# First weights, early splits of the output rows, one column group of the softmax scaling on ScalarE, and gate's half folded into the values

## The chip, the core and the metric

The kernel runs on one core of a Trainium2 chip. Its time is the device time of one execution in microseconds (us). The engines that matter here are TensorE (PE, with its weight loads shown as PEld), VectorE (DVE), ScalarE (ACT), GpSimd (POOL) and SyncE (SP), which issues nearly all DMAs.

## What is computed

One layer of a hybrid encoder on 2048 tokens, a grid of 32 rows by 64 columns, of width 1024, in float32:

```python
h = rmsnorm(x, g)                              # 2048 x 1024
q, k, v, gate = split(h @ w_in, 4, axis=-1)    # w_in: 1024 x 4096
# 16 heads of 64: each token attends to 8 rows x 16 columns of the grid
# around it, with a learned bias per head and offset
s = einsum(q, k_window) * scale + bias         # NEG_INF outside the window
p = softmax(s)
o = einsum(p, v_window)
x = x + (o * silu(gate)) @ w_out               # w_out: 1024 x 1024
return rmsnorm(x, norm_f)
```

silu(gate) is gate/2 times (1 + tanh(gate/2)). The kernel keeps gate times (1 + tanh(gate/2)); the factor one half is applied elsewhere, and the change moves that place.

## The kernel before

**Arithmetic.** Every large product is made of three matmuls: each operand is rounded into a high part and a low part (high minus the rest), and high by high, high by low and low by high are added up in PSUM. So every operand is "split" first: usually ScalarE rounds (`wh`, `h`, `qh`, `gh`, `woh` by a Copy) and VectorE subtracts (`wl`, `l`, `ql`, `gl`, `wol`).

**Stages.** *Stage one* projects the first 1024 tokens. It starts with the values: `load_v0` (L529) and `load_x` bring in blocks of weights (two of 256 columns, a=0 and a=1; a block b holds two rows of blocks k) and of x; `split_v` (L537 the high part, L538 the low part) and `split_to` (L519) split them, and `values_of` (L555) multiplies, block k after block k, into four banks `pv`. The first block k=0 is done in two halves of 256 tokens. The rest of stage one and *stage two* (the other half of the tokens) use a scheme with seven products (L434); parts of stage two's projections are kept back.

*The attention loop* has 32 steps m and a last one. A step handles one pair of heads p and one band of rows T, in the order (p, 0) for eight p, (p, 1) and (p, 2) for eight p each, (p, 3) for eight p. Its instructions are written out in a fixed order, which is the order in each engine's queue. In step m:

1. `begin` sets up loads for later, `feed` emits a first stretch of filling matmuls;
2. `normalise(2m-1)` takes the reciprocal of the row sums (VectorE, L1040) and scales the second pair of column groups of the step before (GpSimd, L1044: two column groups j by two heads s);
3. `split_q` splits the next q (L519, L520), and three "turns" follow: `consume` splits the next item of weights, w_out's pieces in the later half (L194 high, L195 low), and `feed` emits filling matmuls;
4. `tables` adds bias and mask for a new type of row (GpSimd, L987), then one more turn and a last stretch of filling;
5. `turns(m-1)` transposes the probabilities (TensorE, L1101) and copies them out of PSUM (L1077, half on ScalarE, half on VectorE), then come the scores of step m (TensorE L1021, VectorE L1029, ScalarE's exponential with its sum L1035, GpSimd's L1044 for the first pair) and the products with the values (L1123).

**Filling.** `feed(n)` takes n matmuls from `projections()` (the projections kept back, L378 to L382) and, when those are used up, from `outputs()`, which multiplies the gated attention by w_out: per output tile n of 128 rows and half j of the columns 24 matmuls into a bank `po` (L1322 high by high, L1324 low rows by high weights, L1326 high rows by low weights), then `add_rows` adds x (L1220) and squares, and after the second half `finish` brings the root (L1237 on) and the scaling of the final norm (L1252). `amount[m]` is the filling of a step: 28 matmuls, later 53, in the last step 24; the stretches of a step get shares of it. `outputs()` calls `ahead` after each group of three matmuls: it loads rows of gated attention for coming tiles (`load_og`), and splits tile n (`split_og`, ScalarE's `gh` L1187, VectorE's `gl` L1188, two operations of 512 columns each) when its place is near. `clock` counts filling matmuls; a piece that has been loaded is only used when the clock has moved on by a threshold (32 for weights, 28 for rows).

Of the kernel before, what the change touches and what calls it, by code (L numbers as in the profile page):

```python
# [70 lines left out]
def build(ctx, tc, x, xr, xt, wg, rpb, last, w_out, n0, nf, masks, out):  # L71
# [58 lines left out]
    onesr = one.tile([128, 128], F32R, name="onesr")  # L130
    rt = one.tile([128, 16], F32, name="rt")
    g0 = one.tile([128, NK], F32, name="g0")
    accs = [one.tile([128, 512], F32, name=f"acc{i}") for i in range(2)]
# [24 lines left out]
    def load_item(it):  # L158
        kind, a, b = it
        t = raws[it] = raw([128, 512], F32, "raw")  # L160
        asked_at[it] = clock[0]
        if kind == "x":
            nc.sync.dma_start(t, xt[a * 128:(a + 1) * 128, b * 512:(b + 1) * 512])
        elif kind == "w":
            nc.sync.dma_start(t, wg[a[0], :, 512 * b:512 * b + 512])
        else:
            nc.sync.dma_start(t, w_out[a * 128:(a + 1) * 128, b * 512:(b + 1) * 512])
# [38 lines left out]
    def stats(c):  # L206
        ss = rows.pop(c)
        m = tiny.tile([128, 8], F32, name="m")[:, :4]
        nc.vector.tensor_tensor(m, ss[:, 0:8:2], ss[:, 1:8:2], OP.add)
        nc.vector.tensor_scalar(m, m, 1.0 / D, EPS, op0=OP.mult, op1=OP.add)  # L210
        rsqrt(rt[:, 4 * c:4 * c + 4], m, 4)

    dgs = {}
# [48 lines left out]
    AHEAD = 5  # L262
    clock = [0.0]
    freed = set()
    state = dict(used=0, loaded=0, half=-1, done_halves=0, event=0.0)
# [22 lines left out]
    def consume(n, asked=False, turn=False):  # L288
        for _ in range(n):
            load_ahead()  # L290
            if attending[0] and not asked and not turn:
                return
            if state["used"] == len(items) or not may_use(items[state["used"]]):
                return
            if attending[0] and clock[0] - asked_at[items[state["used"]]] < 32 and not asked:
                return
            it = items[state["used"]]
            state["used"] += 1
            use_item(it)
# [88 lines left out]
    def evac_v(u, t, p):  # L388
        v = ev([128, 512], F32, "v")
        nc.scalar.activation(v, p, AF.Copy, scale=rt[:, t:t + 1] if t < 8 else 1.0)  # L390
        dst = vd[u].rearrange("h n d -> n h d")[t * 128:t * 128 + 128]
        written.add(("v", u, t))
        store(("v", u, t), 8, lambda: nc.sync.dma_start(dst, v.rearrange("p (h d) -> p h d", h=4)))
# [136 lines left out]

    def split_v(u, a, b, ks=(0, 1)):
        t = VR[u, a, b].rearrange("p (k c) -> p k c", c=256)
        if a == 0 and ks[0] == 0:
            W[u, b] = wp([128, 2, 512], F32R, "wh"), wp([128, 2, 512], F32R, "wl")
        s, k = slice(a * 256, a * 256 + 256), slice(ks[0], ks[-1] + 1)
        h, l = W[u, b][0][:, k, s], W[u, b][1][:, k, s]
        nc.scalar.activation(h, t[:, k], AF.Copy)  # L537
        nc.vector.tensor_tensor(l, t[:, k], h.bitcast(F32), OP.subtract)  # L538
        if (a, ks[-1]) == (1, 1):
            for a in range(2):  # L540
                del VR[u, a, b]
# [24 lines left out]
    def stage_one():  # L566
# [108 lines left out]
        for b in (1, 2, 3):  # L675
            for a in range(2):
                load_v0(0, a, b, ev([128, 512], F32, "raw") if b == 3 else None)
            for k in (2 * b, 2 * b + 1):
                load("x%d1" % (k // 4 + 1), k % 4)
        for k in range(4):  # L680
# [5 lines left out]
        for k in range(NK):  # L686
            if k == 0:
                for h in range(2):
                    split_to(*(t[:, parts_[h]] for t in X1["B11"][0]), land["x11"][0][:, parts_[h]], gain("x11", 0))
                    if h == 0:  # L690
                        split_v(0, 0, 0, (0,))
                        split_v(0, 1, 0, (0,))
                    values_of(X1, 0, (2 * h, 2 * h + 1), (0,))
                continue
            elif k == 1:
                split_v(0, 0, 0, (1,))
                split_v(0, 1, 0, (1,))
            elif k % 2 == 0:
                split_v(0, 0, k // 2)
                split_v(0, 1, k // 2)  # L700
            f = "x%d1" % (k // 4 + 1)
            split("B" + f[1:], land[f][k % 4], k % 4, f)
            values_of(X1, 0, (0, 1, 2, 3), (k,))
# [82 lines left out]
    def stage_two():  # L786
# [9 lines left out]
        def also(n, i):  # L796
            if n == 0:
                if i == 0:
                    load_ahead()
                    load_e(0, xp)[0]()  # L800
                elif i == 1:
                    load_e(0, xp)[1]()
                    load_masks()
# [166 lines left out]

    def load_e(p, pool_=None):
        def rows(s):
            t = (pool_ or ep)([128, 512], F32, "e")[:, :480]
            E[p, s] = t.rearrange("p (u v) -> p u v", v=32)
            nc.sync.dma_start(t, rpb[2 * p + s])

        return [lambda: rows(0), lambda: rows(1)]
# [59 lines left out]

    def normalise(i):
        st = ST.pop(i)
        nc.vector.reciprocal(st[:, 8:12], st[:, 4:8])  # L1040
        for j, C in enumerate(pairs[i][2]):
            for s in range(2):
                o = 8 + 2 * j + s
                nc.gpsimd.tensor_scalar(X[i, C][s], X[i, C][s], st[:, o:o + 1], 0.5, op0=OP.mult, op1=OP.mult)  # L1044

# [234 lines left out]
    ready = dict(loaded=2, split=1, res=RES_EARLY)  # L1280

    def outputs():
        loaded_at = {1: -1e9}

# [4 lines left out]
        def ahead(k, i=0):  # L1289
            n = ready["loaded"]  # L1290
            if n < tiles and place[n] <= k + 4 and og_ready(n):
                load_og(n)
                loaded_at[n] = clock[0]
                ready["loaded"] += 1
            if ready["res"] < min(squared[0] + RES_BUFS, k + 3, len(turns_)):
                more_rows()
            n = ready["split"]
            near = 2 if quiet[0] else -1
            if n < ready["loaded"] and place[n] <= k + near and clock[0] - loaded_at[n] >= 28 and whole(n):
                split_og(n)  # L1300
# [77 lines left out]
    def begin(m):  # L1378
# [11 lines left out]
        if m == 0:  # L1390
            bias(0, 0, 2)
            later_loads(load_e(order[1][0]), 5, 3)

# [17 lines left out]
    for m in range(cycles + 1):  # L1411
        a = amount[m]
        begin(m)
        feed(a * 0.35)
        if m:
            normalise(2 * m - 1)
        middle(m)
        if m:
            quiet[0] = True
            for k in range(3):  # L1420
                consume(1 + (m == 1), turn=True)
                feed(a * 0.11)
                if k == 1:
# [3 lines left out]
            if quiet[0]:  # L1427
                consume(1, turn=True)
                feed(a * 0.12)
                quiet[0] = False  # L1430
            else:
                feed(a * 0.12)
        else:
            feed(a * 0.45)
        feed(a * 0.2, 8)
        if m:
# [11 lines left out]
        if m:  # L1448
            values(2 * m - 2)
            values(2 * m - 1)  # L1450
        n = next_sums(m)
        if 0 < m and n and order[m][1] < 2:
            for f in load_e(order[n][0]):
                f()
# [52 lines left out]
```

## Time and profile before

| | |
|---|---|
| median of 3 runs | 1062.33 us (1062.28 to 1062.53) |
| profiled execution | 1062.42 us, of which the span of the profile is 1060.6 |
| TensorE busy | 1048.6 us (99%), granted clock 0.9 or more in each slice |
| VectorE / ScalarE / GpSimd busy | 725.7 (68%) / 518.5 (49%) / 312.9 (30%) us |
| normalising on GpSimd, L1044 | 256 instructions, 176.1 us |
| DMA | 207.58 MB, mean 196 GB/s |

"Busy" is the time in which an engine works on an instruction; issuing a DMA or waiting is not counted. In a list of waits a row reads: engine, the waiting group, what released it, the total wait, how often, the longest. In a timeline a row reads: time from the span's start, duration, engine, line of the kernel, operation, output<-inputs, their shapes and types, xN for N instructions of one kind in a row, and in brackets the idle time ahead of it with what released it. A row of a window reads: the window, its length, then the busy time (and number of instructions) of PE, PEld, DVE, ACT and POOL in it, the granted TensorE clock, the busy share of the DMA engines and GB/s. A row of the groups reads: line, engine, operation, shapes, number | busy time, mean ns of one | idle time ahead and its releaser.

### The profile page before, as it was taken

To read this page: it belongs to the slowest core of one execution; us is meant where nothing else is said; L and a number is where in the kernel's file an instruction comes from. 1 tells how busy PE (TensorE), PEld (TensorE's weight loads), DVE (VectorE), ACT (ScalarE), POOL (GpSimd) and SP (SyncE) were. 2 spreads that over 40 slices of the span, in tenths; PEclk is the share of its full clock that TensorE was granted. 3 is DMA by queue.
4 is the path that set the end of the run, shared out by engine and by line. 5 is a ranking of instruction groups with operands and counts; after the bars stand their busy time and mean duration, and the time that the engine had idled before them with its cause. 6 is when DMAs were issued, how large, how long until landed. Compare 5 with 4: busy or idle time off the path is not lost.

```text
span 1060.6 us, 20997 instructions
## 1 busy us (share of the span) xinstructions
PE 1048.6 (99%) x7608; PEld 877.1 (83%) x7608; DVE 725.7 (68%) x1593; ACT 518.5 (49%) x1218; POOL 312.9 (30%) x392
## 2 busy tenths in 40 slices
PE   8999999999999999999999999999999999999997
PEld 6888888887888888888888888888887888888886
DVE  5476888768897625666576667766778777686654
ACT  7645344333343334333265656666767656445422
POOL 0000221322311000000157775665756642213200
PEclk9999999999999999999999999999999999999999
DMA  8733655353635433533798778886987788777352
GB/s 309 227 100 108 190 202 179 126 149 119 184 120 154 120 100 89 170 99 129 234 300 262 239 238 246 269 268 207 297 280 251 222 282 273 255 243 247 105 155 80
DMA packets 129184, 207.58 MB, mean 196 GB/s; under 512 B 11768, under 2 KB 55544, under 8 KB 129080
## 3 DMA queue, kind: packets, MB, share of 16 engines
q1 hardware_dynamic: 128648, 205.84, 62.5%
q8 instruction: 60, 0.98, 0.4%
q10 hardware_dynamic: 432, 0.40, 0.1%
q14 instruction: 44, 0.36, 0.1%
HBM read 147.47 MB, written 58.72 MB: 194 GB/s over the span
## 4 chain that ended last, share of the span: by engine, by line
PE 91%; DVE 4%; issue 1%; POOL 1%; DMA 1%; ACT 0%; SPq 0%; POOLq 0%; DVEq 0%
PE pp L434 30%; PE pv L555 16%; PE s L1021 7%; PE o L1123 7%; PE po L1324 5%; PE po L1326 5%; PE po L1322 5%; PE pp L382 4%; PE pp L378 4%; PE pp L380 4%; PE ph L1101 4%; DVE f L417 1%; POOL x L1044 1%; DMA land<-in_xt_dram 1%; POOL em L987 1%
## 5 line engine op out<-in xcount | busy, mean ns | idle before, releaser
L1044 POOL TENSOR_SCALAR x<-x,st 128x360 f32<-128x360 f32 (+5 forms) x256 | 176.1, 706 | 222.9 <-DVE st L1040 205.0
L434 PE MATMUL pp<-h,f 128*128 128x512 f32 x576 | 186.6, 390 | 0.0
L1035 ACT ACTIVATE x<-x,st 128x360 f32<-128x360 f32 (+5 forms) x256 | 151.3, 593 | 23.7 <-DVE st L1029 23.7
L454 POOL TENSOR_TENSOR tmp<-tmp,rb 128x512 f32<-128x512 f32 x36 | 58.6, 1628 | 270.1 <-DVE tmp L452 209.4
L987 POOL TENSOR_TENSOR em<-e,mk 128x264 f32<-128x264 f32 (+3 forms) x94 | 78.0, 864 | 192.1 <-DMA mk<-in_masks_dram 189.4
L434 PEld LDWEIGHTS pp<-h,f 128*128 128x128 f32 x576 | 108.2, 188 | 22.2
L1029 DVE CUSTOM_DVE_ANT_0 x<-s,em 128x360 f32<-128x360 f32 (+5 forms) x256 | 123.8, 538 | 0.6 <-POOL em L987 0.6
L434 PE MATMUL pp<-t,f 128*128 128x512 f32 x480 | 121.7, 390 | 0.3
L434 PE MATMUL pp<-l,f 128*128 128x512 f32 x288 | 112.2, 389 | 0.0
L434 PEld LDWEIGHTS pp<-t,f 128*128 128x128 f32 x480 | 90.0, 188 | 19.6 <-DVE u L447 1.1
L1324 PE MATMUL po<-woh,gl 128*128 128x512 f32 x252 | 99.2, 394 | 1.5 <-DVE gl L1188 1.5
L1326 PE MATMUL po<-wol,gh 128*128 128x512 f32 x252 | 98.9, 393 | 0.0
L1322 PE MATMUL po<-woh,gh 128*128 128x512 f32 x252 | 98.9, 393 | 0.0
L1077 DVE COPY pta<-ph 120x512 f32<-120x512 f32 (+5 forms) x96 | 57.8, 641 | 55.4 <-PE ph L1101 55.4
L555 PE MATMUL pv<-wh,h 128*128 128x512 f32 x256 | 88.4, 391 | 1.9 <-ACT h L519 1.4
L555 PE MATMUL pv<-wh,l 128*128 128x512 f32 x256 | 88.2, 390 | 0.0
L555 PE MATMUL pv<-wl,h 128*128 128x512 f32 x256 | 88.2, 390 | 0.0
L1077 ACT ACTIVATE pta<-ph 120x512 f32<-120x512 f32 (+5 forms) x96 | 49.7, 558 | 77.0 <-PE ph L1101 76.8
L1123 PEld LDWEIGHTS o<-pta,vt 120*64 120x64 f32 (+2 forms) x1792 | 80.9, 138 | 7.4 <-DVE st L1029 5.4
L1123 PE MATMUL o<-pta,vt 120*64 120x128 f32 (+5 forms) x1792 | 85.3, 253 | 0.0
L417 DVE TENSOR_TENSOR f<-raw,f 128x512 fp32r<-128x512 f32 x90 | 69.7, 775 | 22.4 <-ACT f L416 22.4
L1021 PE MATMUL s<-kt,qh 64*128 64x480 f32 (+5 forms) x512 | 83.0, 372 | 0.5 <-DVE pta L1077 0.5
(157 smaller groups left out, 1959.5 us busy)
## 6 DMA issues: line engine op xcount, KB each, us to landing
raw<-in_wg_dram SPq DMA_DIRECT2D x126, 256.0 KB, 5.0
row<-in_xr_dram SPq DMA_DIRECT2D x32, 256.0 KB, 4.0
vd<-v SPq DMA_DIRECT2D x32, 256.0 KB, 2.4
k_hi<-hi SPq DMA_DIRECT2D x32, 256.0 KB, 2.5
k_lo<-lo SPq DMA_DIRECT2D x32, 256.0 KB, 2.9
sgd<-sg SPq DMA_DIRECT2D x32, 256.0 KB, 4.1
qr<-qd SPq DMA_DIRECT2D x32, 256.0 KB, 5.0
sgt<-sgd SPq DMA_DIRECT2D x32, 256.0 KB, 5.1
```

What stands on the lines that cost most here:

```text
L434: nc.tensor.matmul(B[n, P], t[:, int(m == 2), c], x[k][int(m == 1)], start=P in (1, 6, 5) and k == 0 and m == 0, stop=k == 3 and m == 2, s ...
L555: nc.tensor.matmul(ps[t], a[:, o], b, start=k == 0 and m == 0, stop=k == NK - 1 and m == 2)
L987: (nc.gpsimd if attending[0] or not s else nc.vector).tensor_tensor(sh(t), E[p, s][:, u0 + 4:u1 + 4, v0 + 8:v1 + 8].rearrange("p u (s v) - ...
L1021: nc.tensor.matmul(pst[s], qq[a, qs], kk[a, :r1 - r0, c0:c1].rearrange("p r (s c) -> p s r c", c=8), start=(m == 0), stop=(m == 2))
L1029: nc.vector.tensor_tensor_reduce(X[i, C][s], pst[s], EM[p, ROW_TYPE[T], COL_TYPE[C], s], -1.0, 1e38, OP.add, OP.min, st[:, o:o + 1])
L1035: nc.scalar.activation(X[i, C][s], X[i, C][s], AF.Exp, bias=st[:, o:o + 1], scale=-1.0, accum_out=st[:, 4 + o:5 + o])
L1044: nc.gpsimd.tensor_scalar(X[i, C][s], X[i, C][s], st[:, o:o + 1], 0.5, op0=OP.mult, op1=OP.mult)
L1077: (nc.vector.tensor_copy if h else lambda o, i_: nc.scalar.activation(o, i_, AF.Copy))(t[:k, h, b * 512:b * 512 + w], banks_[b, h][:k, :w])
L1123: nc.tensor.matmul(to.rearrange("d (h q) -> d h q", q=64) if nq > 64 else to, vt[:k, strip, s * 64:s * 64 + 64], t[:k, h, at:at + 64] if n ...
L1322: nc.tensor.matmul(p, gh, woh[q, j], start=(i == 0), stop=False)
L1324: nc.tensor.matmul(p, gl, woh[q, j], start=False, stop=False)
L1326: nc.tensor.matmul(p, gh, wol[q, j], start=False, stop=(i == NK - 1))
```

## The change

There are four parts.

1. *Startup.* The high part of the first half-block of weights a=1 is rounded by VectorE (`tensor_copy`), ahead of x's first half; a=0's stays on ScalarE, behind x. The weights of block b=1 are asked for in halves, with x's block k=2 between the first and the second halves.
2. *Output rows.* `split_rows` splits the next output tile inside a step's turns, in place of a piece of w_out, when the tile's place is within three turns and at least 40 have passed since its load. The clock against which loads are measured, `now`, counts 26 more for each step; the threshold for weights goes from 32 to 36. `ahead` itself splits only when the attention loop has ended. The first stretch of filling of a step becomes 10 matmuls, the others get shares of the remainder.
3. *Normalising.* In the second pair of each step, the column group j=1 is scaled by ScalarE (two Copy activations with a scale per partition) and not by GpSimd.
4. *Gate's half.* The values are scaled by rstd/2 (`rth`, made by two small VectorE operations) instead of rstd, and the normalising scales by 1 in place of 0.5.

Besides, the tables' first bias loads (`load_e`) bring only the rows that the type of row reads: 11 of 15 for the first.

```diff
@@ -129,6 +129,7 @@
     rt = one.tile([128, 16], F32, name="rt")
+    rth = one.tile([128, 8], F32, name="rth")
     g0 = one.tile([128, NK], F32, name="g0")
@@ -158,7 +159,7 @@
         t = raws[it] = raw([128, 512], F32, "raw")
-        asked_at[it] = clock[0]
+        asked_at[it] = now()
         if kind == "x":
@@ -209,6 +210,8 @@
         rsqrt(rt[:, 4 * c:4 * c + 4], m, 4)
+        if c < 2:
+            nc.vector.tensor_scalar(rth[:, 4 * c:4 * c + 4], rt[:, 4 * c:4 * c + 4], 0.5, None, op0=OP.mult)
@@ -261,6 +264,11 @@
     clock = [0.0]
+    runs = [0]
+
+    def now():
+        return clock[0] + 26 * runs[0]
+
     freed = set()
@@ -292,7 +300,7 @@
                 return
-            if attending[0] and clock[0] - asked_at[items[state["used"]]] < 32 and not asked:
+            if attending[0] and now() - asked_at[items[state["used"]]] < 36 and not asked:
                 return
@@ -387,7 +395,7 @@
         v = ev([128, 512], F32, "v")
-        nc.scalar.activation(v, p, AF.Copy, scale=rt[:, t:t + 1] if t < 8 else 1.0)
+        nc.scalar.activation(v, p, AF.Copy, scale=rth[:, t:t + 1] if t < 8 else 0.5)
         dst = vd[u].rearrange("h n d -> n h d")[t * 128:t * 128 + 128]
@@ -528,13 +536,16 @@
-    def split_v(u, a, b, ks=(0, 1)):
+    def split_v(u, a, b, ks=(0, 1), by=None, fresh=True):
         t = VR[u, a, b].rearrange("p (k c) -> p k c", c=256)
-        if a == 0 and ks[0] == 0:
+        if ks[0] == 0 and (a == 0 if by is None else a == 1) and fresh:
             W[u, b] = wp([128, 2, 512], F32R, "wh"), wp([128, 2, 512], F32R, "wl")
...
         h, l = W[u, b][0][:, k, s], W[u, b][1][:, k, s]
-        nc.scalar.activation(h, t[:, k], AF.Copy)
+        if by is None:
+            nc.scalar.activation(h, t[:, k], AF.Copy)
+        else:
+            by.tensor_copy(h, t[:, k])
         nc.vector.tensor_tensor(l, t[:, k], h.bitcast(F32), OP.subtract)
@@ -673,10 +684,13 @@
         for b in (1, 2, 3):
-            for a in range(2):
-                load_v0(0, a, b, ev([128, 512], F32, "raw") if b == 3 else None)
-            for k in (2 * b, 2 * b + 1):
-                load("x%d1" % (k // 4 + 1), k % 4)
+            for j in range(2):
+                for a in range(2):
+                    if b == 1:
+                        load_v0(0, a, b, cols=parts_[j])
+                    elif j == 0:
+                        load_v0(0, a, b, ev([128, 512], F32, "raw") if b == 3 else None)
+                load("x%d1" % (b // 2 + 1), (2 * b + j) % 4)
         for k in range(4):
@@ -686,10 +700,11 @@
                 for h in range(2):
+                    if h == 0:
+                        split_v(0, 1, 0, (0,), nc.vector)
                     split_to(*(t[:, parts_[h]] for t in X1["B11"][0]), land["x11"][0][:, parts_[h]], gain("x11", 0))
                     if h == 0:
-                        split_v(0, 0, 0, (0,))
-                        split_v(0, 1, 0, (0,))
+                        split_v(0, 0, 0, (0,), fresh=False)
                     values_of(X1, 0, (2 * h, 2 * h + 1), (0,))
@@ -797,9 +812,9 @@
                     load_ahead()
-                    load_e(0, xp)[0]()
+                    load_e(0, 0, xp)[0]()
                 elif i == 1:
-                    load_e(0, xp)[1]()
+                    load_e(0, 0, xp)[1]()
                     load_masks()
@@ -968,11 +983,13 @@
-    def load_e(p, pool_=None):
+    def load_e(p, ty, pool_=None):
+        r0, r1 = (4, 15) if ty == 0 else (0, 15)
+
         def rows(s):
...
             E[p, s] = t.rearrange("p (u v) -> p u v", v=32)
-            nc.sync.dma_start(t, rpb[2 * p + s])
+            nc.sync.dma_start(t[:, r0 * 32:r1 * 32], rpb[2 * p + s][:, r0 * 32:r1 * 32])
@@ -1035,13 +1052,16 @@
-    def normalise(i):
+    def normalise(i, both=False):
         st = ST.pop(i)
...
                 o = 8 + 2 * j + s
-                nc.gpsimd.tensor_scalar(X[i, C][s], X[i, C][s], st[:, o:o + 1], 0.5, op0=OP.mult, op1=OP.mult)
+                if both and j:
+                    nc.scalar.activation(X[i, C][s], X[i, C][s], AF.Copy, scale=st[:, o:o + 1])
+                else:
+                    nc.gpsimd.tensor_scalar(X[i, C][s], X[i, C][s], st[:, o:o + 1], 1.0, op0=OP.mult, op1=OP.mult)
@@ -1279,8 +1299,16 @@
+    def split_rows():
+        n = ready["split"]
+        if n < ready["loaded"] and "turn" in ready and place[n] <= ready["turn"] + 3 and now() - late["loaded_at"][n] >= 40 and whole(n) \
+                and sum(1 if hasattr(g, "rearrange") else 2 for g in G.values()) <= 6:
+            split_og(n)
+            ready["split"] += 1
+            return True
+
     def outputs():
-        loaded_at = {1: -1e9}
+        loaded_at = late["loaded_at"] = {0: -1e9, 1: -1e9}
@@ -1290,13 +1318,13 @@
                 load_og(n)
-                loaded_at[n] = clock[0]
+                loaded_at[n] = now()
                 ready["loaded"] += 1
...
             n = ready["split"]
-            near = 2 if quiet[0] else -1
-            if n < ready["loaded"] and place[n] <= k + near and clock[0] - loaded_at[n] >= 28 and whole(n):
+            ready["turn"] = k
+            if ended[0] and n < ready["loaded"] and place[n] <= k + 2 and now() - loaded_at[n] >= 28 and whole(n):
                 split_og(n)
@@ -1389,7 +1417,7 @@
             bias(0, 0, 2)
-            later_loads(load_e(order[1][0]), 5, 3)
+            later_loads(load_e(order[1][0], 0), 5, 3)
@@ -1409,30 +1437,32 @@
     for m in range(cycles + 1):
-        a = amount[m]
+        a = amount[m] - 10
         begin(m)
-        feed(a * 0.35)
+        feed(10)
         if m:
-            normalise(2 * m - 1)
+            normalise(2 * m - 1, True)
         middle(m)
...
             for k in range(3):
-                consume(1 + (m == 1), turn=True)
-                feed(a * 0.11)
+                if not split_rows():
+                    consume(1 + (m == 1), turn=True)
+                feed(a * 0.17)
                 if k == 1:
...
             if quiet[0]:
-                consume(1, turn=True)
-                feed(a * 0.12)
+                if not split_rows():
+                    consume(1, turn=True)
+                feed(a * 0.19)
                 quiet[0] = False
             else:
-                feed(a * 0.12)
+                feed(a * 0.19)
         else:
-            feed(a * 0.45)
-        feed(a * 0.2, 8)
+            feed(a * 0.7)
+        feed(a * 0.3, 8)
         if m:
@@ -1448,9 +1478,10 @@
             values(2 * m - 1)
+        runs[0] += 1
         n = next_sums(m)
         if 0 < m and n and order[m][1] < 2:
-            for f in load_e(order[n][0]):
+            for f in load_e(order[n][0], ROW_TYPE[order[n][1]]):
                 f()
...
     store(("roots",), 8, run_roots)
```

## The prediction

> **What bounds the kernel now.** I read the page's busy times first, then the waits of TensorE, then the timeline at each wait. All times are us.
>
> ```profile
> span 1060.6 us, 20997 instructions
> ...
> PE 1048.6 (99%) x7608; PEld 877.1 (83%) x7608; DVE 725.7 (68%) x1593; ACT 518.5 (49%) x1218; POOL 312.9 (30%) x392
> ```
>
> ```profile
> PE po L1324 <- DVE gl L1188: 1.5, 2, 1.1
> PE pv L555 <- ACT h L519: 1.4, 1, 1.4
> ...
> PE s L1021 <- DVE pta L1077: 0.5, 2, 0.4
> PE pv L555 <- ACT wh L537: 0.5, 1, 0.5
> ```
>
> TensorE is busy for 1048.6 of 1060.6, and all that it waits for inside the run is these six waits, 3.9 in total (the two numbers behind each total are how often and the longest). The changed program holds the same matmuls in the same order, so there is no TensorE work to save. Everything that the edits do to VectorE, ScalarE, GpSimd and the DMA queues counts only as far as it removes, lengthens or adds a wait of TensorE. I go through the waits by place. The sum is made against the profiled execution, 1062.42 with 1.82 outside its span; the median shown is 1062.33, 0.09 less. A difference of 0.2% (2.1) is about what a measurement of this kernel can tell from no change.
>
> **The first weights.** The profile of the first 15 us:
>
> ```profile
> 4.26 0.72 ACT L537 ACTIVATE wh<-raw 128x256 fp32r<-128x256 f32 x2
> 4.71 0.76 DVE L538 TENSOR_TENSOR wl<-raw,wh 128x256 fp32r<-128x256 f32 x2
> 5.03 0.74 PE L555 MATMUL pv<-wh,h 128*128 128x512 f32 x2 [0.49 <-ACT wh L537]
> ...
> 7.87 0.63 ACT L537 ACTIVATE wh<-raw 128x512 fp32r<-128x512 f32 x1 [0.33 <-DMA raw<-in_wg_dram]
> ...
> 9.93 0.63 ACT L537 ACTIVATE wh<-raw 128x512 fp32r<-128x512 f32 x1 [1.43 <-DMA raw<-in_wg_dram]
> ...
> 11.41 1.41 ACT L519 ACTIVATE h<-land,g 128x512 fp32r<-128x512 f32 x2 [0.85 <-DMA land<-in_xt_dram]
> ...
> 12.18 1.20 PE L555 MATMUL pv<-wh,h 128*128 128x512 f32 x4 [1.38 <-ACT h L519]
> ...
> 14.13 1.07 PE L555 MATMUL pv<-wh,l 128*128 128x512 f32 x4
> ```
>
> ```profile
> 10.00:12.00 2.00, 0.80 (x4) 0.34 (x2) 0.69 (x1) 1.15 (x2) 0.00 (x0) 1.00 0.97 325
> ```
>
> VectorE rounding one of the two first weight blocks takes 0.36 (half of 0.72) off ScalarE ahead of the first matmul at 5.03. VectorE pays with one more operation ahead of the second pair of matmuls, which needs both low parts: rounding, low part, x's low part, low part, four times some 0.38 to 0.48 from the landing at about 4, is 5.6, where 4.71 plus 0.76 is 5.47 now. Either way the gain is gone at 12.18, where TensorE waits 1.38 for block k=2 of x. That wait is the DMA's: the engines are 97% busy (last but one number of the window's row) at 325 GB/s, and k=2 has three landings, the two weight blocks (7.87, 9.93) and x (11.41). In the change these weights are asked for in halves and x's k=2 between them, so x lands about two 128 KB pieces earlier. But the rounding for k=2 (L537) still reads the whole blocks, both halves, and stands ahead of x on ScalarE. The bytes ahead of the last of the three are the same, so the last landing stays near 11.4, only it is now the second weight block. Behind it ScalarE has the block's rounding, 0.63, and then x, where it had x alone: **+0.63**. Ends: a DMA stretch faster by what x gains (256 KB at 325 GB/s is 0.8) less what the order costs gives -0.7; halves that move slower give +1.1. I take +0.63, the row's own number.
>
> By the Trainium skill ("DMA: Bandwidth & Descriptors", Measured, under Bandwidth) a 64 KB transfer takes 0.95 and a 1 MB one 6.15; drawn as a line, an estimate from that page, each transfer has 0.6 of its own, and the two added ones would cost 1.2 more if they were paid in line. The window's row speaks against that, with the engines 97% busy and hence the next transfer always at hand; the sum would be +0.75 by the page and is -0.45 by the row.
>
> **The output rows, split ahead.** The two waits for gl (L1188) are the splits of output tiles 1 and 2.
>
> ```profile
> 793.90 0.18 DVE L1040 RECIPROCAL st<-st 128x4 f32<-128x4 f32 x1 [0.59 <-ACT x L1035]
> ...
> 794.42 1.02 DVE L520 SCALAR_TENSOR_TENSOR ql<-qr,qh 128x512 fp32r<-128x512 f32 x1 [0.34 <-ACT qh L519]
> ...
> 794.81 1.14 ACT L1187 ACTIVATE gh<-ograw 128x512 fp32r<-128x512 f32 x2
> ...
> 795.97 1.67 DVE L1188 TENSOR_TENSOR gl<-ograw,gh 128x512 fp32r<-128x512 f32 x2
> ...
> 797.09 0.51 PE L1324 MATMUL po<-woh,gl 128*128 128x512 f32 x1 [0.40 <-DVE gl L1188]
> ```
>
> ```profile
> 809.69 0.50 PE L1322 MATMUL po<-woh,gh 128*128 128x512 f32 x1
> ...
> 811.30 0.50 PE L1324 MATMUL po<-woh,gl 128*128 128x512 f32 x1 [1.10 <-DVE gl L1188]
> ```
>
> Matmuls follow each other every 0.23 ((1.07 - 0.39)/3 in the row of 14.13, a single one showing 0.39), so the one at 811.30 is 1.38 late. In the change tile 2 is split in the step before, right behind tile 1, and this wait goes: **-1.38** (end: -0.5, if w_out's pieces, put off to here, hold VectorE). The wait at 797.09 stays, for tile 1 can't be split earlier: w_out's piece ahead of it leaves ScalarE's queue, but the two new normalisations enter it. Their price:
>
> ```profile
> L1035 ACT ACTIVATE x<-x,st 128x360 f32<-128x360 f32 x64 | 37.4, 586 | 12.4 <-DVE st L1029 12.4
> ```
>
> An exponential over the same tile takes 0.586 with its sum, gh over 512 columns 0.57 (half of 1.14); a plain scaling of 360 columns I take at 0.45, ends 0.35 and 0.59. Two make 0.9. They wait for the reciprocal (794.08), so qh comes at 795.0, gh from 795.5, and VectorE's ql and gl end between 797.1 and 797.7: **+0.3** (-0.1 to +0.6).
>
> The Trainium skill ("GPSIMD Engine Reference", Specifications) has GpSimd and VectorE share their way into SBUF when VectorE reads two SBUF inputs. The trace agrees: ql takes 1.02 above, where GpSimd normalises, and 0.66 below, at 824.61. With half of these normalisations gone from GpSimd, that rule alone would make this term 0.
>
> **w_out's last pieces.** The turns that now split rows are turns that w_out's pieces lose; the last three are split in the step at 822, where turn 3 already needs them.
>
> ```profile
> 823.04 0.61 ACT L519 ACTIVATE qh<-qr 128x512 fp32r<-128x512 f32 x1
> ...
> 823.92 0.69 DVE L1220 TENSOR_TENSOR y<-po,xr 128x512 f32<-128x512 f32 x1 [1.34 <-PE po L1326]
> ...
> 824.53 0.17 DVE L1040 RECIPROCAL st<-st 128x4 f32<-128x4 f32 x1
> ...
> 824.61 0.66 DVE L520 SCALAR_TENSOR_TENSOR ql<-qr,qh 128x512 fp32r<-128x512 f32 x1
> ...
> 825.19 0.68 DVE L195 TENSOR_TENSOR wol<-raw,woh 128x512 fp32r<-128x512 f32 x1
> ```
>
> Here the new wait is on ScalarE: its normalisations wait for the reciprocal, that waits in VectorE's queue for y, and y for TensorE. Queued behind them are qh (now 823.04), then pieces 5 to 7 of w_out. From 824.7: normalise to 825.6, qh to 826.2, piece 5 high to 826.8, low to 827.5; its first use is 15 matmuls into the turn that begins at 823.7, at 827.1, the low part at 827.6. Piece 6 is due 0.7 later and is behind a square of 0.6: **+0.3** (0 to +0.7).
>
> **One column group on ScalarE, where VectorE's queue is tight.**
>
> ```profile
> 837.80 0.61 ACT L519 ACTIVATE qh<-qr 128x512 fp32r<-128x512 f32 x1
> ...
> 838.45 0.79 DVE L520 SCALAR_TENSOR_TENSOR ql<-qr,qh 128x512 fp32r<-128x512 f32 x1 [1.23 <-ACT qh L519]
> ...
> 839.16 1.57 DVE L1188 TENSOR_TENSOR gl<-ograw,gh 128x512 fp32r<-128x512 f32 x2
> ...
> 842.36 1.41 DVE L1252 SCALAR_TENSOR_TENSOR y<-y,st,acc 128x512 f32<-128x512 f32 x2
> ...
> 843.69 1.75 DVE L1077 COPY pta<-ph 120x512 f32<-120x512 f32 x3
> 844.42 0.75 PE L1021 MATMUL s<-kt,qh 64*128 64x480 f32 x4 [0.38 <-DVE pta L1077]
> ```
>
> From 838.45 on VectorE runs without a break (ql, gl, the root, the scaling, the copies) and TensorE waits for the first copy. VectorE's chain starts from qh, and qh moves back by the two normalisations, 0.9. VectorE wins back some 0.35 by a less busy GpSimd (1.57 for two gl; 0.66 for ql at 824.61 against 0.79): **+0.55** (0 to +1.0). In the steps without output work the copies start as soon as TensorE's transposes allow, and ScalarE idles ahead of them; what hides the 0.9 there is that idle time.
>
> The other copy wait is a burst of two tiles' roots and scalings in one step:
>
> ```profile
> 947.49 2.73 DVE L1252 SCALAR_TENSOR_TENSOR y<-y,st,acc 128x512 f32<-128x512 f32 x4
> ...
> 951.47 0.41 PE L1021 MATMUL s<-kt,qh 64*128 64x288 f32 x2 [0.17 <-DVE pta L1077]
> ```
>
> In the late steps the change emits normalise, split and roots some 1 to 2 earlier, since the first stretch of filling is 10 matmuls instead of 0.35 of 53. Only one of the two roots is then due here, the other falls in the next step, where the same shift leaves it room: **-0.4** (-0.6 to 0; 0.17 is the idle time shown, 1.4 is what leaves VectorE).
>
> GpSimd's own lateness shows in one step:
>
> ```profile
> 742.06 4.11 POOL L1044 TENSOR_SCALAR x<-x,st 128x480 f32<-128x480 f32 x4 [2.17 <-DVE st L1040]
> ...
> 744.90 1.84 PE L1101 MATMUL ph<-ident,x 64*120 64x64 f32 x42
> ```
>
> ```profile
> 785.66 1.50 PE L1101 MATMUL ph<-ident,x 64*120 64x64 f32 x44
> ```
>
> Four scalings there end at 746.17, after the transposes began; 42 of 44 take 1.84 and the rest come behind, where 44 take 1.50 elsewhere. With two of the four on ScalarE it goes: **-0.45** (to 0).
>
> Taken at nothing: the two small operations for rth (a reciprocal on 128x4 shows 0.18) and the half moved into v's scale, in a stretch where TensorE waits for nothing; the shorter loads of e, fewer bytes on SP's queue; loads of q, k and w_out that change places by a few entries on SP's queue, landing well before use. The end after the last matmul is untouched.
>
> Sum: 0.63 - 0.45 + 0.3 - 1.38 + 0.3 + 0.55 - 0.4 = -0.45, so 1062.42 becomes 1061.97, and the median 1062.33 becomes **1061.9**.
>
> **The rivals.** *Faster.* x's early landing decides at k=2 (the weights come as fast), and VectorE gains enough from a quieter GpSimd that no new wait appears: -0.7 - 0.45 - 0.1 - 1.38 + 0 + 0.1 - 0.5 is -3.0, so 1059.3. For it speaks that 1.4 of waiting is there to be had at 12.18, against it the whole-block rounding. Chance 0.25.
>
> *Slower.* ScalarE's queue now stands behind VectorE's reciprocal in each of 32 steps, and its copies of the transposes come late. It decides where copies start over some 1.5 after the transposes (at 843.69, 1.9 after, TensorE waited 0.38). If eight of the steps pay 0.4 each, 3.2 are added: -0.45 + 3.2 is +2.75, so 1065.1. Against it: no step but those named has copies that late now. Chance 0.15.
>
> *The gain only moves*: two splits in a row at 797 push y and w_out back there and the 1.38 returns as waits; the sum is then +0.9, 1063.3, still within 0.2%. It shares 0.6 with the forecast.
>
> **How the numbers follow.** Faster 0.25, within 0.2% 0.6, slower 0.15. The range leaves out a tenth on each side: from the faster rival, 1059.3, to somewhat short of the slower one, 1064.0.
>
> **What would show it.** Right: no wait for gl near 811, one near 797 of 0.4 to 1.0; the k=2 matmuls at 12.5 to 13.0 behind a rounding of weights; new short waits for wol or woh near 827; a longer wait for pta near 844, none near 951. Wrong: k=2 at 11.5; waits for pta in many steps; TensorE waits of a kind not listed here.

## The result and the profile after

| | us, median | lowest to highest | ratio to before, 95% interval |
|---|---|---|---|
| before, five runs beside it | 1062.28 | 1061.06 to 1062.53 | |
| changed | 1070.80 | 1070.04 to 1072.82 | 1.0089 (1.0074 to 1.0103) |

The change makes the kernel 8.5 us slower; the forecast was 1061.9. The profiled execution took 1072.82, the longest of the five, 10.4 more than the profiled execution of the kernel before. From the page of the changed kernel (busy time per engine):

```profile
span 1071.0 us, 20949 instructions
...
PE 1052.8 (98%) x7608; PEld 877.9 (82%) x7608; DVE 734.3 (69%) x1596; ACT 547.3 (51%) x1281; POOL 264.2 (25%) x328
```

GpSimd has lost 48.7 of work, as the change means it to, ScalarE has 28.8 more, and VectorE, which got next to nothing new, has 8.6 more. That last number is the trail. The waits of TensorE in the changed kernel (engine and group, what released it, total, times, longest):

```profile
PE s L1038 <- DVE pta L1097: 4.2, 3, 2.6
PE po L1352 <- DVE gl L1208: 1.5, 1, 1.5
...
PE po L1354 <- DVE wol L196: 1.1, 1, 1.1
PE s L1038 <- DVE lo L373: 1.0, 1, 1.0
PE pv L566 <- ACT h L527: 0.9, 1, 0.9
PE s L1038 <- ACT pta L1097: 0.8, 1, 0.8
PE s L1038 <- DVE y L1240: 0.7, 1, 0.7
```

10.2 of waiting in place of 3.9, and all but the startup's 0.9 of it is for work of VectorE and ScalarE in the attention loop (`lo` is the low part of a new k, `y` the output rows with x added). Where it lies shows when the start of the transposes of each step is compared between traces. The last two columns are what the distance to the kernel before grows by in that step, worked out from the starts; "alone" is the run with the output rows' part only (e8 below).

| transposes start, before | start, changed | changed adds | rows' part alone adds |
|---|---|---|---|
| 560.72 | 562.08 | +1.43 | -0.03 |
| 612.82 | 614.70 | +0.50 | +0.07 |
| 758.72 | 764.50 | +3.94 | -0.01 |
| 799.86 | 806.71 | +1.15 | -0.75 |
| 814.92 | 823.40 | +1.62 | -1.66 |
| 828.34 | 838.26 | +1.44 | +0.05 |
| 841.81 | 852.42 | +0.70 | -0.03 |
| 856.79 | 867.98 | +0.58 | -0.01 |
| 968.84 | 979.31 | -0.63 | -0.63 |
| the startup and 22 other steps | | -0.2 | -0.6 |

The losses stand in eight rows; no other step adds over 0.2. In the attention loop GpSimd makes fifteen sets of tables (bias plus mask for a new type of row, L1004). Seven of the eight rows lie beside five of these sets, at 544, 596, 745, 801 and 835 in the changed kernel: a set runs past the start of one step's transposes, and the loss shows there or in the row behind it. The step of the eighth row, 856.79, makes no tables. The other ten sets cost TensorE next to nothing. The worst, from the timeline of the changed kernel, and below it two more of the same kind:

```profile
743.82 1.08 ACT L1062 ACTIVATE x<-x,st 128x360 f32<-128x360 f32 x2 [0.90 <-DVE st L1057]
744.80 0.62 ACT L527 ACTIVATE qh<-qr 128x512 fp32r<-128x512 f32 x1
745.20 7.27 POOL L1004 TENSOR_TENSOR em<-e,mk 128x360 f32<-128x360 f32 x6
745.46 1.17 DVE L528 SCALAR_TENSOR_TENSOR ql<-qr,qh 128x512 fp32r<-128x512 f32 x1 [1.74 <-ACT qh L527]
746.55 4.36 DVE L196 TENSOR_TENSOR wol<-raw,woh 128x512 fp32r<-128x512 f32 x3
750.83 1.74 DVE L1097 COPY pta<-ph 120x512 f32<-120x512 f32 x3
751.57 0.76 PE L1038 MATMUL s<-kt,qh 64*128 64x480 f32 x4 [2.64 <-DVE pta L1097]
...
801.23 7.73 POOL L1004 TENSOR_TENSOR em<-e,mk 128x360 f32<-128x360 f32 x6
802.58 5.65 DVE L1208 TENSOR_TENSOR gl<-ograw,gh 128x512 fp32r<-128x512 f32 x4
...
834.61 7.27 POOL L1004 TENSOR_TENSOR em<-e,mk 128x360 f32<-128x360 f32 x6
835.96 4.37 DVE L196 TENSOR_TENSOR wol<-raw,woh 128x512 fp32r<-128x512 f32 x3
```

The same place in the timeline of the kernel before:

```profile
742.36 2.28 DVE L195 TENSOR_TENSOR wol<-raw,woh 128x512 fp32r<-128x512 f32 x3
745.65 0.69 DVE L1077 COPY pta<-ph 120x512 f32<-120x512 f32 x1 [1.01 <-PE ph L1101]
746.14 5.48 POOL L987 TENSOR_TENSOR em<-e,mk 128x360 f32<-128x360 f32 x6
```

Three splits of w_out took 2.28, beside GpSimd's scalings, and were done before the tables began. Now they take 4.36, 1.45 each, beside the tables, and `ql` ahead of them takes 1.17 in place of 0.66; the copies of the transposes stand behind them in VectorE's queue; TensorE waits 2.64. The tables pay as well, 7.27 for six in place of 5.48. It shows in the groups by shape as well (busy, mean ns of one), before and changed:

```profile
L987 POOL TENSOR_TENSOR em<-e,mk 128x480 f32<-128x480 f32 x16 | 17.3, 1105 | 0.0
L195 DVE TENSOR_TENSOR wol<-raw,woh 128x512 fp32r<-128x512 f32 x16 | 12.3, 808 | 0.0
```

```profile
L1004 POOL TENSOR_TENSOR em<-e,mk 128x480 f32<-128x480 f32 x16 | 22.2, 1412 | 0.0
L196 DVE TENSOR_TENSOR wol<-raw,woh 128x512 fp32r<-128x512 f32 x16 | 16.0, 1039 | 0.7 <-ACT woh L195 0.7
```

A second loss hangs on the first. Windows of 1 us behind the wait of 2.64 (the third number from the end is the granted clock):

```profile
752.00:753.00 1.00, 1.00 (x12) 0.84 (x9) 1.00 (x5) 0.00 (x0) 0.47 (x1) 1.00 0.94 325
753.00:754.00 1.00, 1.00 (x10) 0.83 (x6) 1.00 (x7) 0.94 (x3) 0.00 (x0) 0.58 1.05 425
754.00:755.00 1.00, 1.00 (x10) 0.78 (x10) 1.00 (x5) 1.00 (x5) 0.00 (x0) 0.50 1.02 400
755.00:756.00 1.00, 1.00 (x16) 1.00 (x14) 1.00 (x6) 1.00 (x4) 0.00 (x0) 0.50 1.04 399
756.00:757.00 1.00, 1.00 (x20) 1.00 (x20) 0.82 (x4) 1.00 (x5) 0.94 (x2) 0.71 1.06 404
```

The clock is halved for about 3.4 (from 753.2, by the share of its first slice), beginning 1.6 after TensorE's work resumed. That is the remainder of the +3.94: 2.64 of waiting and 1.3 of slow matmuls (the 56 products with the values that follow take 3.77 here and 2.67 before). The trace has one more such stretch, from 811.2 to 814.6.

### The profile page after: what moved, and what is told of

Its sections match the earlier page's. It is cut to its first block, busy times and chain, and to the rows that moved or that the text cites. A ratio compares the mean times of both kernels' runs of the same rounds, so it can differ in the third digit from the quotient of the medians.

```text
span 1071.0 us, 20949 instructions
## 1 busy us (share of the span) xinstructions
PE 1052.8 (98%) x7608; PEld 877.9 (82%) x7608; DVE 734.3 (69%) x1596; ACT 547.3 (51%) x1281; POOL 264.2 (25%) x328
## 4 chain that ended last, share of the span: by engine, by line
PE 86%; DVE 6%; ACT 2%; issue 2%; DMA 2%; SPq 1%; DVEq 0%; ACTq 0%
PE pp L442 29%; PE pv L566 16%; PE o L1143 7%; PE s L1038 7%; PE po L1350 5%; PE po L1352 5%; PE po L1354 5%; PE pp L390 3%; PE ph L1121 3%; PE pp L386 3%; PE pp L388 3%; DVE f L425 1%; DMA raw<-in_wg_dram 1%; DVE x L1046 1%; ACT x L1052 1%
## 5 line engine op out<-in xcount | busy, mean ns | idle before, releaser
L1064 POOL TENSOR_SCALAR x<-x,st 128x480 f32<-128x480 f32 (+5 forms) x192 | 110.6, 593 | 279.4 <-DVE st L1057 257.1
L1004 POOL TENSOR_TENSOR em<-e,mk 128x264 f32<-128x264 f32 (+3 forms) x94 | 94.8, 1043 | 194.0 <-PE pp L442 188.9
```

Of the source, the lines that this page charges most:

```text
L1004: (nc.gpsimd if attending[0] or not s else nc.vector).tensor_tensor(sh(t), E[p, s][:, u0 + 4:u1 + 4, v0 + 8:v1 + 8].rearrange("p u (s v) - ...
```

## The experiments

Theory A: GpSimd, relieved of two scalings, adds the tables while VectorE still splits, both are slowed, and copies come late. Rival B: the early splits and shifted turns do it. Rival C: ScalarE's queue, in which q now stands behind a reciprocal, does it by itself. All ratios are to runs of the kernel before on the same chip; e1 to e4, e5 to e8 and e9 ran on three chips, on which the kernel before took 1061.85, 1061.81 and 1062.04.

| run | us, median | ratio, 95% interval |
|---|---|---|
| e1 all scalings on GpSimd | 1059.44 | 0.9977 (0.9967 to 0.9986) |
| e2 ScalarE scales unless tables follow | 1060.34 | 0.9986 (0.9977 to 0.9995) |
| e3 ScalarE's scaling and gate's half alone | 1077.25 | 1.0143 (1.0129 to 1.0157) |
| e4 startup alone | 1061.52 | 0.9996 (0.9987 to 1.0005) |
| e5 column group's scaling left out | 1059.44 | 0.9978 (0.9969 to 0.9987) |
| e6 ScalarE scales, GpSimd multiplies too | 1066.08 | 1.0038 (1.0024 to 1.0052) |
| e7 tables by memset | 1060.64 | 0.9988 (0.9979 to 0.9997) |
| e8 output rows' part (with shorter loads and gate's half) | 1058.82 | 0.9970 (0.9959 to 0.9982) |
| e9 e1 and first weights rounded in halves | 1058.31 | 0.9966 (0.9952 to 0.9979) |

**e1: all scalings on GpSimd.**

```diff
-            normalise(2 * m - 1, True)
+            normalise(2 * m - 1)
```

> The changed kernel with all four scalings of the second pair back on GpSimd; everything else of the change stays. Theory A (GpSimd, relieved of two scalings, starts the bias tables while VectorE still splits, both are slowed, and the copies of the transposes come late): the waits near 749, 808, 837 and 855 go and the time falls to 1060.5 to 1062.5. Rival B (the early splits of output rows and the shifted turns pack VectorE's work into the time of the tables): little is undone, 1068 to 1071. Rival C (ScalarE's queue, which now stands behind VectorE's reciprocal, delays q in every step): as A.

1059.44, below the expected interval and below the kernel before. B falls: the rest of the change gains 2.4. C stands beside A.

**e2: ScalarE scales only where no tables follow.**

```diff
-            normalise(2 * m - 1, True)
+            due_tables = m < cycles and (order[m][0], ROW_TYPE[order[m][1]], 0, 0) not in EM
+            normalise(2 * m - 1, not due_tables)
```

> The changed kernel, with the column group on ScalarE only in those steps that compute no bias tables. Theory A: the waits in the steps with tables go (near 550, 749, 802 to 810, 837), the one near 855, a step without tables, stays at about 1: 1061 to 1063.5. Rival C: the delay of q is the cause, and half of the steps still have it: 1065 to 1068. Rival B: 1068 to 1071.

1060.34, 0.7 below the interval of theory A. In the list of waits one is left inside the run beside that of the startup:

```profile
PE s L1038 <- DVE pta L1097: 1.0, 1, 1.0
```

It lies at 841.64, in the step without tables that the expectation named (855 in the changed kernel). ScalarE keeps its scalings in every step without tables, and the run takes 0.9 more than e1, of which 0.55 stands in this step. C as it was put, by which these steps alone should have cost 3 and more, is out; what a late q does in the steps with tables is left to e7.

**e3: ScalarE's scaling without the other parts.** The kernel before with `rth`, `evac_v` and `normalise(2 * m - 1, True)` of the diff.

> The kernel before with two parts of the change alone: the column group on ScalarE in the second pair of every step, and gate's half in the values. Theory A: the step at 745 pays about 3 as in the changed kernel, those near 800 and 815 some 1 to 3 more, and the granted clock falls after the longest stall: 1066 to 1070. Rival B: about the time before, 1061 to 1063. Rival C: 1064 to 1068, with waits in steps with and without tables.

1077.25: all three intervals were too low, A's by 7. The profiled execution took 1074.98, the shortest of the four. The waits:

```profile
PE s L1024 <- DVE pta L1083: 3.9, 3, 2.6
PE po L1330 <- DVE gl L1194: 2.9, 2, 2.5
PE s L1024 <- DVE lo L368: 2.1, 1, 2.1
PE po L1328 <- ACT gh L1193: 1.5, 2, 1.1
```

The step near 750 waits as in the changed kernel (2.65 against 2.64). Larger are the wait for `lo` at 549, 2.06 against 0.99, with a halved clock behind it, and the waits for the splits of output rows: for tile 1, beside the tables, 0.37 for `gh` at 803.8 and 2.46 for `gl` at 804.7; for tile 2, a step later, 1.13 and 0.40 at 821 to 823, where the kernel before waits 1.1. The clock is halved three times. So the parts are not additive: beside ScalarE's scaling the others are worth 6.4 by the medians (1077.25 to 1070.80), by themselves 2.4 (e1). The two profiled executions lie only 2.2 apart (1074.98 and 1072.82), so the traces show where a third of the 6.4 comes from; the remainder isn't shown.

**e4: the startup alone.** The kernel before with the three hunks on `split_v`, the loads and the first rounding.

> The kernel before with the startup part alone: VectorE rounds the first half-block of one weight, and the weights of block b=1 are asked for in halves with x's block k=2 between. The changed kernel's trace has the k=2 matmuls at 11.92 (12.18 before), so -0.3 against the time before, 1061.6 to 1062.3; as forecast (rounding of whole blocks ahead of x) +0.6, 1062.7 to 1063.2.

1061.52, 0.33 less than before, which the interval doesn't separate from nothing. The first matmul of k=2 came at 12.15 (12.18 before), with a wait of 1.02 in place of 1.38. The timeline of ScalarE:

```profile
10.86 0.63 ACT L538 ACTIVATE wh<-raw 128x512 fp32r<-128x512 f32 x1 [0.32 <-DMA raw<-in_wg_dram]
11.39 1.32 ACT L519 ACTIVATE h<-land,g 128x512 fp32r<-128x512 f32 x2
```

x is rounded at 11.39 as before, now with no idle time ahead: it is held by the rounding of the weights, of which the second block landed at 10.86, and not by its own landing.

**e5: the column group's scaling left out**, by `pass` in place of ScalarE's activation; part of the probabilities stays unnormalised.

> The changed kernel with the scaling of the second pair's column group j=1 left out (done by no engine, so that part of the probabilities stays unnormalised). GpSimd reaches the tables as early as in the changed kernel, and ScalarE takes q on time. If early tables alone make the waits: 1065 to 1069. If it takes both (tables early and VectorE's splits late, so that these fall inside the tables): by the trace of before, VectorE's three splits run from 742.4, the tables would start at 743.4, the copies could start at 746.0 where they are needed at 746.3: no wait of over 0.5 in the steps with tables, 1059 to 1062.

1059.44, as e1. But it did not put the tables beside the splits, as was expected. GpSimd and VectorE in its timeline:

```profile
741.91 3.03 POOL L1064 TENSOR_SCALAR x<-x,st 128x480 f32<-128x480 f32 x2 [2.15 <-DVE st L1057]
742.22 2.28 DVE L196 TENSOR_TENSOR wol<-raw,woh 128x512 fp32r<-128x512 f32 x3
744.92 5.50 POOL L1004 TENSOR_TENSOR em<-e,mk 128x360 f32<-128x360 f32 x6
```

With q on time VectorE's splits fall beside the two scalings, and there it is GpSimd that waits: two scalings take 3.03 where the changed kernel's two take 1.32, three splits 2.28. The tables begin when the splits are done. One wait of 0.66 is left beside tables, at 800, for a copy on ScalarE. So the run does not show what early tables alone would cost, only that taking work from GpSimd does no harm while VectorE stays on time.

**e6: both engines on the column group.** ScalarE scales, GpSimd multiplies the same tiles by 1 behind it.

```diff
                 if both and j:
                     nc.scalar.activation(X[i, C][s], X[i, C][s], AF.Copy, scale=st[:, o:o + 1])
+                    nc.gpsimd.tensor_scalar(X[i, C][s], X[i, C][s], 1.0, 1.0, op0=OP.mult, op1=OP.mult)
```

> The changed kernel with ScalarE's scalings kept and GpSimd multiplying the same column group by 1 behind them: q is as late as in the changed kernel, the tables start as late as before. If the delay of q on ScalarE alone makes the waits: 1067 to 1071. If it takes both: only the last of VectorE's splits falls into the tables, the step near 749 waits some 1.4 in place of 2.6, that near 855 its 1.0 as before: 1062 to 1066.

1066.08, just above the expected interval. From the timeline:

```profile
744.26 3.54 DVE L196 TENSOR_TENSOR wol<-raw,woh 128x512 fp32r<-128x512 f32 x3
744.66 6.83 POOL L1004 TENSOR_TENSOR em<-e,mk 128x360 f32<-128x360 f32 x6
```

The splits fall beside the tables less fully, 3.54 for three, and TensorE waits 1.42 at 747.03, the 1.4 expected. The clock stays full. With q as late as in the changed kernel (`ql` waits 1.73 for it) half of the loss is gone, 4.3 in place of 8.5; what differs in this step is that the tables begin 0.4 behind the splits and not 1.35 ahead of them.

**e7: the tables by memset**, with ScalarE still scaling; bias and mask are left out.

```diff
             EM[p, ty, cty, s] = t
+            if attending[0]:
+                nc.gpsimd.memset(t, 0.0)
+                continue
```

> The changed kernel with the bias tables of the attention loop set to zero by a memset on GpSimd (bias and mask are left out); ScalarE still scales its column group and q is still late. Theory A (the collision of VectorE's splits with the tables' additions): VectorE's splits take 0.7 again, the wait near 749 goes (copies at 748.1, needed at 748.2), those near 550, 809 and 837 too, some 0.4 stays near 802 and 1.0 near 855: 1060 to 1062. Rival C (the late q by itself): 1066 to 1070.

1060.64. From the timeline:

```profile
743.21 2.30 POOL L1005 MEMSET em<- 128x360 f32 x6
743.50 0.69 DVE L528 SCALAR_TENSOR_TENSOR ql<-qr,qh 128x512 fp32r<-128x512 f32 x1 [1.73 <-ACT qh L527]
744.11 1.89 DVE L196 TENSOR_TENSOR wol<-raw,woh 128x512 fp32r<-128x512 f32 x3
745.92 1.74 DVE L1100 COPY pta<-ph 120x512 f32<-120x512 f32 x3
```

q is as late as in the changed kernel (`ql` waits 1.73, there 1.74) and GpSimd works beside most of the splits, but only writes. The splits take 0.63 each (0.68 by their own records, which overlap a little), and the copies start in time. It holds throughout the attention loop: of the splits of 128x512 (w, w_out and output rows), 39 with GpSimd idle take 0.68 to 0.69 in the changed kernel, 26 that lie beside tables take 0.75 to 1.60, half of them over 1.35, and in this run 13 beside a memset take 0.68 to 0.69. The waits for `lo`, `wol` and `y` are gone, that for `pta` is the 1.0 of the step without tables, and `gl` waits 0.3. The collision of two engines that both read two tiles is the cause of the large waits; the late q brings it about. Without the collision ScalarE's scaling costs 1.2 (1060.64 against 1059.44 in e1): in the comparison of steps the rows of 799.86, 828.34 and 856.79 add 0.75, 0.35 and 0.56 more than in e1, and that of 758.72 adds 0.36 less.

**e8: the output rows' part.** The changed kernel with startup and normalising as before.

> The kernel before with the early splits of output rows, their thresholds and turns, the shorter loads of e and gate's half; startup and normalising as before. Theory A: the two waits for gl (0.4 and 1.1) go, the burst of roots at 951 eases by 0.5, no other comes: 1062.1 less 2.1 is 1060.0, 1059.3 to 1060.6. As forecast for these parts (+0.3 -1.38 +0.3 -0.4, so -1.2): 1060.9.

1058.82, 3.0 less than before, below both expected values and 0.9 more of a gain than theory A's 2.1; 0.36 of it stands in the startup, which this run leaves as it was, so that much is variation of the landings. Of its waits one is left behind the startup:

```profile
PE s L1031 <- DVE pta L1090: 0.4, 1, 0.4
```

and the split of output tiles 1 and 2 clears the tables:

```profile
794.94 3.16 DVE L1201 TENSOR_TENSOR gl<-ograw,gh 128x512 fp32r<-128x512 f32 x4
798.50 5.95 POOL L997 TENSOR_TENSOR em<-e,mk 128x360 f32<-128x360 f32 x6
```

Four operations take 3.16 here and 5.65 in the changed kernel. With the startup's part added (e1) the gain was 2.4 and not 3.0, and the startup's part alone (e4) gave 0.33: these runs show no gain of that part that is clear of their spread.

**e9: the first weights rounded in halves, too**, on top of e1.

```diff
             elif k % 2 == 0:
-                split_v(0, 0, k // 2)
-                split_v(0, 1, k // 2)
+                for h in range(2):
+                    split_v(0, h, k // 2, (0,) if k == 2 else (0, 1))
+            elif k == 3:
+                for h in range(2):
+                    split_v(0, h, 1, (1,))
```

> The changed kernel with all scalings on GpSimd, and with the weights of block b=1 rounded in halves too, as they are asked for: the first half ahead of x's block k=2, the second ahead of k=3. In the run without this, ScalarE rounds two whole blocks from 9.87 to 11.27 and x's k=2 comes behind, so TensorE waits 0.6 at 11.4. If the whole-block rounding is what holds x back, that wait goes: 0.3 to 0.6 less than 1059.4, 1058.8 to 1059.2, with the k=2 matmuls at 11.4 to 11.7. If the landings hold it back, the wait stays at 0.5 or more and the time too.

1058.31, the lowest of all and below the expected interval. The timeline of ScalarE:

```profile
9.35 0.72 ACT L527 ACTIVATE h<-land,g 128x512 fp32r<-128x512 f32 x1 [0.76 <-DMA land<-in_xt_dram]
9.98 0.40 ACT L546 ACTIVATE wh<-raw 128x256 fp32r<-128x256 f32 x1
10.86 0.42 ACT L546 ACTIVATE wh<-raw 128x256 fp32r<-128x256 f32 x1 [0.48 <-DMA raw<-in_wg_dram]
```

x's k=2 is rounded at 9.35, as soon as it lands, 2.0 earlier than in the kernel before, and the matmuls of k=2 start at 10.68 without a wait, earlier than the 11.4 to 11.7 expected. Against e1's median this is 1.1 less, against e8's 0.5; those were measured on other chips, and the intervals of the ratios overlap. The trace places it: up to the first transposes of the attention loop the profiled run gains 1.47 on the kernel before, where e1 gains 0.01 and e8 0.36.

## Why the prediction was wrong, point by point

*The step that failed* is the pricing of VectorE's operations beside GpSimd. The prediction took 0.66 to 0.8 for a split, from rows in which GpSimd scales or rests, and counted a relieved GpSimd as a gain (-0.45 at 744.9, 0.35 at 844). It did not ask what GpSimd does next. In the steps with tables it goes straight on to the additions, and a split beside these takes 1.45. Where the additions are replaced by writes (e7), the kernel takes 1060.64, within the forecast's range: the other terms, rightly sized or not, come out at -1.2 together, where -0.45 was forecast. The prediction also moved q back by 0.9; it moved by about 2 in the step near 749 (`qh` at 744.80, with 1.85 of delay from earlier steps taken off 742.95, against 740.95), since the two scalings also wait for the reciprocal, which waits for `sg`. So VectorE's splits left the scalings, beside which GpSimd gives way (e5), and met the tables, beside which VectorE waits.

*"What hides the 0.9 there is that idle time"* holds in steps without tables (e2: one wait) and fails in those with them: 1.43, 0.50 and 3.94 stand in steps that the sum took at nothing or at -0.45. These three, the first stretch of half clock among them, are 5.9 of the 10.9 by which the sum missed the profiled execution (1072.82 against 1061.97).

*797, tile 1: +0.3.* +1.15 was measured; the wait is 1.50, for a `gl` beside the tables. Without ScalarE's scaling it goes entirely (e8, -0.75): with w_out's pieces out of the way the split is early enough. With the scaling and without the collision the step adds -0.04 (e7), so the prediction was right that the new scalings use up that gain.

*811, tile 2: -1.38.* Right as a mechanism: that wait is gone, and e8 gains 1.66 there. In the changed kernel the step pays 0.68 for VectorE's `y` and 0.79 for a copy on ScalarE, which both come behind the four slow splits of 802.58, and the second clock stretch.

*w_out's last pieces: +0.3.* A wait of 1.15 came, and the step added 1.44. The queue was read rightly: `qh` comes at 834.18, 825.7 with the 8.48 of earlier delay taken off, where 825.6 was forecast, and without the collision the step adds 0.38 (e7). The remainder is the three pieces, which take 4.37 beside the tables. Without ScalarE's scaling it is +0.05 (e8).

*844: +0.55.* Right: the wait grew from 0.38 to 1.06, and the step by 0.58, in a place without tables. e2 and e7 have it too.

*951: -0.4.* Right, -0.63, and in every run with the rows' part.

*744.9: -0.45.* The gain is there when the collision is not: the step adds -0.37 in e7. The changed kernel has it too (the transposes take 1.50) and pays 3.9 behind it.

*k=2 of x: +0.63.* Wrong in sign: the wait fell from 1.38 to 0.89, and the matmuls came at 11.92, 0.26 earlier. The reason given for its price, that rounding whole blocks stands ahead of x, is what e4 and e9 show. But the last weight landed at about 10.1 in the changed kernel, and not at 11.4, so both roundings fit ahead of that. The two added transfers made nothing later: x, rounded at 11.16, was there before the 11.41 of the kernel before.

*The rivals.* The faster one said 1059.3; the parts that it relied on do give 1059.4 and 1058.8 (e1, e8) once ScalarE's scaling is taken out. The slower one, 1065.1, was right in its sign and wrong in its mechanism: it had ScalarE's copies late in eight steps, and without the collision ScalarE's scaling costs 1.2 in all (e7 against e1). That eight rows lost is luck: only four of TensorE's waits are for copies, three of them VectorE's.

*The shared way into SBUF.* The prediction took it from the Trainium skill ("GPSIMD Engine Reference", Specifications) and held that the term at 797 might be 0 by it. The traces bear the sharing out, but the prediction applied it to the scalings that go and not to the additions that move. Its two rows do not separate the cases either: the `ql` of 0.66 at 824.61 also runs beside a scaling, which begins at 824.86. The Trainium skill ("SBUF — State Buffer", SBUF: two separate sides) says that whichever of the two starts first holds the shared pair for a whole instruction and the other is blocked. The trace agrees beside the tables: 0.63 to 0.68 of its own and some 0.8 of waiting is the 1.45 of a split, and six tables take 7.27, which is 5.48 and about three splits of 0.6. Beside scalings it does not: in the kernel before a scaling that starts at 742.06 takes 1.44 in place of 0.66, and the split that starts at 742.36, behind it, takes its usual 0.68. In e5, too, a split takes 0.76 there and a scaling 1.5. So there it is mostly GpSimd that pays, also where it has started first; why is not shown.

## What to carry to other kernels

When work is taken from an engine, ask what that engine will start earlier, and what will then run beside it: two instructions that read two SBUF tiles each, one on GpSimd and one on VectorE, cost each other time: here a split of VectorE's took twice as long, and a set of six tables of GpSimd's a third longer. Look up the price of an operation in the row whose neighbour is the one that it will have after the change. And split a change into its parts: three of these four, without the fourth, gain 2.4, and with the rounding moved to the order of the loads 3.7 (1058.31 against 1062.04).

## What the runs showed of the hardware

The granted clock fell to one half for about 3.4 behind each wait of TensorE of 2.06 to 2.65 (the changed kernel once, e3 three times), beginning 0 to 1.6 after the work resumed, and once behind waits of 0.68 and 0.79 within 2; not behind single waits of 1.38, 1.42 or 1.50, nor behind 1.13 and 0.40 within about 2 (e3) or 0.44 and 0.79 within 2 (e6). The Trainium skill ("TensorE: Matmul & The Clock Gate", Part 1: The HAM clock gate) has the array go to half clock after an idle window of about 3.4 that runs free of the kernel. The length of the slow stretch agrees; here waits shorter than that window were enough. One such stretch cost 1.3 of the 3.94 above, so a wait of over 2 is dearer than it looks. The changed kernel's runs spread over 2.8, those of the kernel before over 1.5; their mean clocks, 0.995 to 0.998, suggest that the number of such stretches differs from run to run, which the traces, one for each kernel, can't show.
